# A state-space branch moved behind each step's evacuation, with a staging tile for its cosine product, two recurrence buffers and a setup in smaller portions

## The chip, the cores and the metric

The kernel runs on one core of a Trainium2 chip. The metric is the time of one execution on the device in microseconds (us). Five engines work side by side, each through a queue of its own, in order: PE (TensorE: matmuls into PSUM), DVE (VectorE), ACT (ScalarE), POOL (GpSimd), and SP (SyncE), which here issues every DMA.

## What is computed

One layer of a streaming encoder: 1024 positions of 1024 channels in float32. An input projection feeds two mixers, a diagonal state-space model (S5) and a gated short convolution. Cut to what matters:

```python
proj = jnp.einsum('bsd,dn->bsn', x, w_in) + b_in
u, h, c_gate, b_gate, gate_a, gate_b = jnp.split(proj, [o1, o2, o3, o4, o5], axis=-1)
y_a = s5_ssm(u, ...)                      # 32 groups of 16 channels, 64 complex states each
g = jax.nn.gelu(y_a)
y_a = g * jax.nn.sigmoid(jnp.einsum('bsc,ce->bse', g, glu_w) + glu_b)
y_a = jnp.einsum('bsc,cd->bsd', y_a, w_ssm_out)
z = causal_depthwise_conv(c_gate * h, conv_w)
y_b = jnp.einsum('bsc,cd->bsd', b_gate * z, w_conv_out)
merged = jax.nn.sigmoid(gate_a) * y_a + jax.nn.sigmoid(gate_b) * y_b
x = layer_norm(ALPHA * x + jnp.einsum('bsd,de->bse', merged, w_o), ln1_g, ln1_b)
hid = jax.nn.silu(jnp.einsum('bsd,df->bsf', x, w_gate)) * jnp.einsum('bsd,df->bsf', x, w_up)
x = layer_norm(ALPHA * x + jnp.einsum('bsf,fd->bsd', hid, w_down), ln2_g, ln2_b)
```

The state of the S5 branch follows `x[t] = a * x[t-1] + B u[t]` with complex `a`, and `y = Re(C x) + D u`.

## The kernel before

**Matmuls.** Every operand is split into a rounded part and a remainder (`hi`, `lo`), and three products of them stand for one (L180 to L182). The large products use a seven-product scheme (Strassen's) on 2 x 2 blocks: a `Pair` of weight blocks gives seven *steps*, each of 12 matmuls of 128 x 512, into four PSUM banks. `Step` holds what belongs to a step: `add` (the sum of two weight blocks, on POOL unless told otherwise), `split` (two copies on ACT, the remainder on DVE), `mm` (the matmuls), and `after` (`Pair.ev`, the evacuation of what has become complete, on ACT, DVE and POOL).

**Order of the work.** All of it is written out by hand; nothing is reordered later. `run` (L310) walks over the steps. At step s it issues the add of step s+4, the split of step s+3, then a portion of each generator in the list `bg` that is due, then the matmuls of step s and its evacuation. A generator's `yield n` says that its next portion comes n steps later. Steps 0 to 111 are the input projection, 112 to 127 the convolution's output projection, 128 to 135 the gate of the S5 branch, 136 to 151 its output projection, and the feed-forward part follows.

**The branch.** The S5 branch lives in generators, beside steps 12 to 127:

- `setup` (L461) computes the tables of the transition `a` in many small DVE operations on 128 x 32 and 128 x 288 elements; `exp_to` is an exponential that is used twice. Its scratch `scr` lies in the tiles with the tags w, ws, z and zs.
- `mats(cc)`, `rot(cc)` and `flow(cc)` work on chunk cc, four groups of channels, cc = 0 to 7. `mats` builds matrices: B (`bst`), Cp, four transposes into the small PSUM tile `pst`, and the kernel product into the small PSUM tile `pk` (L648), copied into K, from which eight DMAs fill the matrix T. `rot` makes a table of cosines C and one of sines S.
- `flow(cc)` is the recurrence: a product into the small PSUM tile `psw` (L710); `w`, its copy by ACT; `ws`, w with its halves swapped by two DMAs; w becomes psw times C on DVE and ws becomes ws times S on POOL; their sum goes through a scan into z (L729); z is rotated back in the same way with `zs` (L733 to L736); the output product `psy` (L739 to L742) uses T and z, and its copy `yn` is stored. Then `s["y"]` is set, on which later chunks wait.
- `gelu(tl)` follows two chunks each.

There are two small PSUM buffers (tag sm, L604), used in turn by pst, pk, psw and psy. The staging ring `stage` (tag st, L338) has four places and is used by evacuations too.

**The end of the branch.** The last flow calls `load_v` (L747), which loads the convolution's result into the tiles z, zs, ws and bp. At the end of step 111, `begin_b` (L913) runs all generators on (`spin`, L1349) until these loads have been issued, and then splits the eight parts of v, which step 112 multiplies. `begin_glu` does the same ahead of step 128 until no generator is left.

Of the kernel before, what the change touches and what calls it, by code (L numbers as in the profile page):

```python
# [15 lines left out]
P = 128  # L16
# [31 lines left out]
def kernel(  # L48
# [256 lines left out]
    def flush():  # L305
        todo, later[:] = later[:], []
        for f in todo:
            f()

    def run(lo, hi):  # L310
        for s in range(lo, hi):
            for f in steps[s].pre:
                f()
            if s + 4 < len(steps) and steps[s + 4].add:
                steps[s + 4].add(eng=V if steps[s + 4].addv else G)
            if s + 3 < len(steps) and steps[s + 3].split:
                steps[s + 3].split()
            for it in list(bg):
                if it[1] <= s:
                    try:  # L320
                        it[1] = s + max(1, next(it[0]) or 1)
                    except StopIteration:
                        bg.remove(it)
            steps[s].mm()
            flush()
            for f in steps[s].mid + steps[s].after:
                f()

    def start(gen, s=0):
        bg.append([gen, s])  # L330
# [121 lines left out]
    def stile(shape, tag, nm, bufs=1, dt=F32):  # L452
        return nonlocal_state["p"].tile(shape, dt, tag=tag, name=nm, bufs=bufs)
# [7 lines left out]
    def setup():  # L461
# [10 lines left out]
        sMim = tb["sMim"] = stile([P, NG, 8], "sMim", "sMim")  # L472
        E8 = tb["E8"] = stile([P, NG], "E8", "E8")
        ph8 = tb["ph8"] = stile([P, 2, NG], "ph8", "ph8")
        scr = [stile([P, 4 * P], t, f"scr_{t}") for t in ("w", "ws", "z", "zs")]
        used = [0] * 4

        def carve(*shape):
            n = int(np.prod(shape))
            i = min(i for i in range(4) if used[i] + n <= 4 * P)  # L480
            t = scr[i][:, used[i] : used[i] + n]
            used[i] += n
            return t.rearrange("p (a b) -> p a b", a=shape[0]) if len(shape) == 2 else t
# [9 lines left out]
        def exp_to(o, y):  # L493
            m, r, q = carve(NG), carve(NG), carve(NG)
            ts(r, y, -100.0, 90.0, ALU.max, ALU.min)
            ts(m, r, LOG2E, MAGIC, ALU.mult, ALU.add)
            ts(m, m, MAGIC, -127.0, ALU.subtract, ALU.max)
            V.tensor_scalar_min(m, m, 128.0)
            V.scalar_tensor_tensor(r, m, -LN2_1, r, ALU.mult, ALU.add)
            V.scalar_tensor_tensor(r, m, -LN2_2, r, ALU.mult, ALU.add)  # L500
            V.tensor_scalar_mul(q, r, 1.0 / 5040.0)
            for c in (1.0 / 720.0, 1.0 / 120.0, 1.0 / 24.0, 1.0 / 6.0, 0.5, 1.0):
                V.scalar_tensor_tensor(q, q, c, r, ALU.add, ALU.mult)
            ts(it, m, 127.0, 8388608.0, ALU.add, ALU.mult)
            V.scalar_tensor_tensor(o, q, 1.0, it.bitcast(F32), ALU.add, ALU.mult)
            yield 1
# [10 lines left out]
        mul(E[:, :, 3:5], E[:, :, 1:3], E[:, :, 2:3].to_broadcast([P, NG, 2]))  # L517
        mul(E[:, :, 5:9], E[:, :, 1:5], E[:, :, 4:5].to_broadcast([P, NG, 4]))
        V.tensor_copy(E8, E[:, :, 8])
        th, hh, hl = carve(NG), carve(NG), carve(NG)  # L520
        mul(th, li, dt)
        V.tensor_scalar_mul(hl, th, 4097.0)
# [14 lines left out]
        add(phh, phh, tm[:, 2])  # L537
        add(phh, phh, tm[:, 3])
        wrap(phh, th)
        add(phl, pr[:, 3], pr[:, 2])  # L540
        add(phl, phl, pr[:, 1])
        add(phl, phl, pr[:, 0])
# [14 lines left out]
        yield 1  # L557
        mul(nLre, nLre, E)
        mul(Lim, Lim, E)
        den, fr, fi, nr, tp = carve(NG), carve(NG), carve(NG), carve(NG), carve(NG)  # L560
        mul(den, lr, lr)
        mul(tp, li, li)
# [49 lines left out]
    def mats(cc):  # L612
# [34 lines left out]
        for g in range(4):  # L647
            PE.matmul(pk[0:16, g, :], B[:, g, 7, :], Cp[:, g, 0:8, :].rearrange("p n c -> p (n c)"),  # L648
                      start=True, stop=True)
        K = stile([16, 4, P], "yn", f"K{cc}")  # L650
        S.activation(K, pk[0:16], AF.Copy)
        for g in range(4):
            V.scalar_tensor_tensor(K[:, g, 0:16], ident[0:16, 0:16], tb["dss"][:, g0 + g : g0 + g + 1],
# [49 lines left out]
    def flow(cc):  # L703
# [8 lines left out]
        S.activation(w, ps, AF.Copy)  # L712
        ws = stile([P, 4, P], "ws", f"ws{cc}")
        swap(ws, w)
        s["sin"] = True
        yield 2
        c = slice(0, 127)
        mul(ws[:, :, c], ws[:, :, c], s["S"], G)
        mul(w[:, :, c], ps[:, :, c], s["C"])
        yield 1  # L720
        add(w[:, :, c], w[:, :, c], ws[:, :, c])
        while cc and "y" not in st[cc - 1]:
            yield 1
        z = stile([P, 4, P], "z", f"z{cc}")
        zs = stile([P, 4, P], "zs", f"zs{cc}")
        V.memset(zs[:, :, 0:1], 0.0)
        S.activation(zs[:, :, 1:P], tb["E8"][:, 4 * cc : 4 * cc + 4, None].to_broadcast([P, 4, 127]), AF.Copy)
# [6 lines left out]
        mul(z[:, :, c], z[:, :, c], s["C"])  # L734
        yield 1
        sub(z[:, :, c], z[:, :, c], zs[:, :, c])  # L736
        yield 3
        ps = small(f"psy{cc}")
        for g in range(4):  # L739
            PE.matmul(ps[:, g, :], s["T"][:, g], s["UT"][:, g], start=True, stop=False)  # L740
# [157 lines left out]
    def load_v(k):  # L898
        if k not in vrs:
            if k == 2:  # L900
                vrs[k] = epi.tile([P, 10, P], F32, tag="zE", name=f"vr{k}")[:, 0:8].rearrange("p a b -> p (a b)")
            elif k == 3:
                vrs[k] = wring.tile([P, KT, P], F32, tag="raw", name=f"vr{k}", bufs=4).rearrange("p a b -> p (a b)")
            else:
                vrs[k] = [stile([P, 4, P], t, f"vr_{t}").rearrange("p a b -> p (a b)")
                          for t in (("z", "zs"), ("ws", "bp"))[k]]
                for h in range(2):
                    nc.sync.dma_start(vrs[k][h], v_d[k, :, half(h)])
                return
            nc.sync.dma_start(vrs[k], v_d[k])  # L910
            vrs[k] = [vrs[k][:, half(h)] for h in range(2)]
# [736 lines left out]
```

## Time and profile before

| | |
|---|---|
| median of 3 runs | 1306.01 us (1303.51 to 1306.93) |
| the profiled execution's own time | 1304.74 us |
| its span, first to last instruction | 1302.9 us |
| mean granted clock of PE | 0.981 |
| moved by DMA | 148.75 MB, mean 114 GB/s |

The profile is of one execution. It gives busy times by engine, the waits (engine and line that waited, engine and line that ended the wait, then the sum in us, how often, and the longest), a timeline (start and duration in us, engine, line, operation, output <- inputs, and in brackets the idle time ahead and what ended it), and windows (start and end, their length, then the busy time and count of PE, of PE's weight loads, of DVE, ACT and POOL, then PE's granted clock, the share of the DMA engines and GB/s). Queue rows name the queue, the size of a transfer and the median time from issue to landing. A PE that stands still between two stretches of dense matmuls shows as idle time ahead of a matmul.

### The profile page before, as it was taken

How to read it: one execution, taken by the hardware profiler on the slowest of the kernel's cores; microseconds unless marked ns; L12 is line 12 of the kernel's file. 1: busy time of each engine (PE TensorE's matmuls, PEld its weight loads, DVE VectorE, ACT ScalarE, POOL GpSimd, SP SyncE). 2: the span in 40 equal slices, each digit the busy share in tenths (PEclk: the TensorE clock that was granted, in tenths of full speed). 3: DMA queues.
4: the chain of work that ended last, by engine and by line, in shares of the span. 5: the costliest groups of instructions: out<-in, count | busy, mean ns of one | idle time of the engine just before them, and what ended most of it. 6: DMA issues, size and time to landing. Idle time of an engine off the chain costs nothing. (4 is left out here: it accounts for less than half of the span.)

```text
span 1302.9 us, 16504 instructions
## 1 busy us (share of the span) xinstructions
PE 1210.6 (93%) x5365; PEld 979.4 (75%) x5365; DVE 860.4 (66%) x1321; ACT 765.4 (59%) x1320; POOL 777.8 (60%) x577
## 2 busy tenths in 40 slices
PE   6788899899899999999879999999999997999984
PEld 4566687777687888888658888888888875877764
DVE  6988688786676675689984444444444445566888
ACT  5645767788786252243435555555555567777871
POOL 5826878696861135123876565566556547585856
PEclk9899999999999999999989999999999998999998
DMA  5221342444456536124214323222215349420012
GB/s 196 78 88 45 110 122 82 128 157 142 131 151 230 195 116 237 38 97 162 81 49 153 104 92 98 73 73 97 95 52 162 97 137 360 143 64 1 1 49 81
DMA packets 95414, 148.75 MB, mean 114 GB/s; under 512 B 16736, under 2 KB 48480, under 8 KB 95072
## 3 DMA queue, kind: packets, MB, share of 16 engines
q1 hardware_dynamic: 95328, 147.70, 35.2%
q8 instruction: 43, 0.70, 0.2%
q14 instruction: 43, 0.35, 0.1%
HBM read 106.11 MB, written 36.18 MB: 109 GB/s over the span
## 5 line engine op out<-in xcount | busy, mean ns | idle before, releaser
L180 PE MATMUL ps_f<-x1h,wl_f 128*128 128x512 f32 x616 | 241.5, 392 | 12.1 <-DVE wl_f L115 7.7
L181 PE MATMUL ps_f<-x1l,wh_f 128*128 128x512 f32 x616 | 240.6, 391 | 2.1 <-DVE x1l L115 2.1
L182 PE MATMUL ps_f<-x1h,wh_f 128*128 128x512 f32 x616 | 240.5, 390 | 0.0
L180 PEld LDWEIGHTS ps_f<-x1h,wl_f 128*128 128x128 f32 x616 | 116.1, 189 | 39.0 <-issue 8.5
L181 PEld LDWEIGHTS ps_f<-x1l,wh_f 128*128 128x128 f32 x616 | 116.1, 188 | 26.7 <-DVE x1l L115 2.7
L182 PEld LDWEIGHTS ps_f<-x1h,wh_f 128*128 128x128 f32 x616 | 116.0, 188 | 24.3
L1478 PE MATMUL pe<-rBh,rAl 128*128 128x512 f32 x297 | 119.0, 401 | 15.4 <-ACT rBh L138 6.4
L115 DVE TENSOR_TENSOR wl_f<-t_f,hp 128x512 fp32r<-128x512 f32 x92 | 62.9, 684 | 88.8 <-ACT hp L137 88.8
L1479 PE MATMUL pe<-rBl,rAh 128*128 128x512 f32 x297 | 116.8, 393 | 0.6 <-DVE rBl L115 0.6
L1480 PE MATMUL pe<-rBh,rAh 128*128 128x512 f32 x297 | 116.5, 392 | 0.0
L180 PE MATMUL ps_gt<-xh,wl_gt 128*128 128x512 f32 x224 | 90.5, 404 | 3.9 <-DVE ec_hc L112 1.4
L182 PE MATMUL ps_gt<-xh,wh_gt 128*128 128x512 f32 x224 | 88.8, 396 | 0.0
L181 PE MATMUL ps_gt<-xl,wh_gt 128*128 128x512 f32 x224 | 88.5, 395 | 0.0
L106 POOL TENSOR_TENSOR tB<-B,B 128x512 f32<-128x512 f32 x55 | 71.8, 1307 | 27.9 <-DVE rBl L115 16.3
L106 POOL TENSOR_TENSOR tA<-A,A 128x512 f32<-128x512 f32 x54 | 69.8, 1297 | 29.9 <-DVE rAl L115 7.4
L106 POOL TENSOR_TENSOR t_f<-raw_f,raw_f 128x512 f32<-128x512 f32 x62 | 83.5, 1347 | 6.6 <-DVE wl_f L115 6.6
L1478 PEld LDWEIGHTS pe<-rBh,rAl 128*128 128x128 f32 x297 | 56.2, 189 | 35.4 <-ACT rBh L138 11.4
L138 ACT ACTIVATE wh_f<-t_f 128x512 fp32r<-128x512 f32 x92 | 57.4, 624 | 32.0 <-PE ps_f L182 31.9
L137 ACT ACTIVATE hp<-t_f 128x512 fp32r<-128x512 f32 x92 | 55.3, 601 | 31.9 <-POOL t_f L106 30.1
L109 POOL TENSOR_TENSOR sgf<-sgf,eb_f 128x512 f32<-128x512 f32 x21 | 27.6, 1313 | 70.7 <-ACT sgf L1183 70.7
L1479 PEld LDWEIGHTS pe<-rBl,rAh 128*128 128x128 f32 x297 | 56.3, 190 | 12.3 <-DVE rBl L115 1.3
L1480 PEld LDWEIGHTS pe<-rBh,rAh 128*128 128x128 f32 x297 | 56.3, 190 | 11.3
(414 smaller groups left out, 3270.1 us busy)
## 6 DMA issues: line engine op xcount, KB each, us to landing
raw_f<-in_wgu SPq DMA_DIRECT2D x45, 512.0 KB, 3.9
h_d<-hid SPq DMA_DIRECT2D x44, 256.0 KB, 2.4
B<-in_wd SPq DMA_DIRECT2D x44, 256.0 KB, 6.1
A<-h_d SPq DMA_DIRECT2D x44, 256.0 KB, 5.8
raw_gt<-in_w SPq DMA_DIRECT2D x16, 512.0 KB, 4.1
s_d<-sg SPq DMA_DIRECT2D x32, 256.0 KB, 2.5
sgd<-s_d SPq DMA_DIRECT2D x16, 512.0 KB, 3.6
raw_hc<-in_w SPq DMA_DIRECT2D x8, 512.0 KB, 4.5
```

What stands on the lines that cost most here:

```text
L106: eng.tensor_tensor(o, a, b, op)
L109: eng.tensor_tensor(o, a, b, ALU.mult)
L115: eng.tensor_tensor(o, a, b, ALU.subtract)
L137: S.activation(hp, raw, AF.Copy)
L138: S.activation(hi, raw, AF.Copy)
L180: PE.matmul(ps, self.lo[:, k, :], xh[:, k, :], start=first and k == 0, stop=False, skip_group_check=True)
L181: PE.matmul(ps, self.hi[:, k, :], xl[:, k, :], start=False, stop=False, skip_group_check=True)
L182: PE.matmul(ps, self.hi[:, k, :], xh[:, k, :], start=False, stop=last and k == 3, skip_group_check=True)
L1478: PE.matmul(ps, al[:, c], bh, start=kp == 0, stop=False)
L1479: PE.matmul(ps, ah[:, c], bl, start=False, stop=False)
L1480: PE.matmul(ps, ah[:, c], bh, start=False, stop=kp == NK - 1)
```

## The change

Five edits, all in the S5 branch and in the loop that issues it:

1. In `run`, the portions of `bg` are issued behind the matmuls and the evacuation of step s, no longer ahead of them.
2. In `flow`, the cosine product follows psw at once, in the same portion, and goes into a tile `wc` of the staging ring; before, it overwrote w two steps later. The sum reads wc and ws and writes w.
3. z gets two buffers, and the scan of a chunk waits for `rotated` (the last chunk's rotation back has been issued) in place of `y`. The pause ahead of psy is four steps, before three.
4. Five pauses more in `setup`, counting the one in `exp_to` twice.
5. K lies in the staging ring, no longer in a tile of its own.

```diff
--- before.py
+++ after.py
@@ -315,16 +315,16 @@
                 steps[s + 4].add(eng=V if steps[s + 4].addv else G)
             if s + 3 < len(steps) and steps[s + 3].split:
                 steps[s + 3].split()
+            steps[s].mm()
+            flush()
+            for f in steps[s].mid + steps[s].after:
+                f()
             for it in list(bg):
                 if it[1] <= s:
                     try:
                         it[1] = s + max(1, next(it[0]) or 1)
                     except StopIteration:
                         bg.remove(it)
-            steps[s].mm()
-            flush()
-            for f in steps[s].mid + steps[s].after:
-                f()
 
     def start(gen, s=0):
         bg.append([gen, s])
@@ -472,7 +472,7 @@
         sMim = tb["sMim"] = stile([P, NG, 8], "sMim", "sMim")
         E8 = tb["E8"] = stile([P, NG], "E8", "E8")
         ph8 = tb["ph8"] = stile([P, 2, NG], "ph8", "ph8")
-        scr = [stile([P, 4 * P], t, f"scr_{t}") for t in ("w", "ws", "z", "zs")]
+        scr = [stile([P, 4 * P], t, f"scr_{t}", 2 if t == "z" else 1) for t in ("w", "ws", "z", "zs")]
         used = [0] * 4
 
         def carve(*shape):
@@ -498,6 +498,7 @@
             V.tensor_scalar_min(m, m, 128.0)
             V.scalar_tensor_tensor(r, m, -LN2_1, r, ALU.mult, ALU.add)
             V.scalar_tensor_tensor(r, m, -LN2_2, r, ALU.mult, ALU.add)
+            yield 1
             V.tensor_scalar_mul(q, r, 1.0 / 5040.0)
             for c in (1.0 / 720.0, 1.0 / 120.0, 1.0 / 24.0, 1.0 / 6.0, 0.5, 1.0):
                 V.scalar_tensor_tensor(q, q, c, r, ALU.add, ALU.mult)
@@ -517,6 +518,7 @@
         mul(E[:, :, 3:5], E[:, :, 1:3], E[:, :, 2:3].to_broadcast([P, NG, 2]))
         mul(E[:, :, 5:9], E[:, :, 1:5], E[:, :, 4:5].to_broadcast([P, NG, 4]))
         V.tensor_copy(E8, E[:, :, 8])
+        yield 1
         th, hh, hl = carve(NG), carve(NG), carve(NG)
         mul(th, li, dt)
         V.tensor_scalar_mul(hl, th, 4097.0)
@@ -537,6 +539,7 @@
         add(phh, phh, tm[:, 2])
         add(phh, phh, tm[:, 3])
         wrap(phh, th)
+        yield 1
         add(phl, pr[:, 3], pr[:, 2])
         add(phl, phl, pr[:, 1])
         add(phl, phl, pr[:, 0])
@@ -557,6 +560,7 @@
         yield 1
         mul(nLre, nLre, E)
         mul(Lim, Lim, E)
+        yield 1
         den, fr, fi, nr, tp = carve(NG), carve(NG), carve(NG), carve(NG), carve(NG)
         mul(den, lr, lr)
         mul(tp, li, li)
@@ -647,7 +651,7 @@
         for g in range(4):
             PE.matmul(pk[0:16, g, :], B[:, g, 7, :], Cp[:, g, 0:8, :].rearrange("p n c -> p (n c)"),
                       start=True, stop=True)
-        K = stile([16, 4, P], "yn", f"K{cc}")
+        K = stage(f"K{cc}").rearrange("p (g k) -> p g k", g=4)[0:16]
         S.activation(K, pk[0:16], AF.Copy)
         for g in range(4):
             V.scalar_tensor_tensor(K[:, g, 0:16], ident[0:16, 0:16], tb["dss"][:, g0 + g : g0 + g + 1],
@@ -712,16 +716,16 @@
         S.activation(w, ps, AF.Copy)
         ws = stile([P, 4, P], "ws", f"ws{cc}")
         swap(ws, w)
-        s["sin"] = True
+        c = slice(0, 127)
+        wc = stage(f"wc{cc}").rearrange("p (g k) -> p g k", g=4)
+        mul(wc[:, :, c], ps[:, :, c], s["C"])
         yield 2
-        c = slice(0, 127)
         mul(ws[:, :, c], ws[:, :, c], s["S"], G)
-        mul(w[:, :, c], ps[:, :, c], s["C"])
-        yield 1
-        add(w[:, :, c], w[:, :, c], ws[:, :, c])
-        while cc and "y" not in st[cc - 1]:
+        yield 1
+        add(w[:, :, c], wc[:, :, c], ws[:, :, c])
+        while cc and "rotated" not in st[cc - 1]:
             yield 1
-        z = stile([P, 4, P], "z", f"z{cc}")
+        z = stile([P, 4, P], "z", f"z{cc}", 2)
         zs = stile([P, 4, P], "zs", f"zs{cc}")
         V.memset(zs[:, :, 0:1], 0.0)
         S.activation(zs[:, :, 1:P], tb["E8"][:, 4 * cc : 4 * cc + 4, None].to_broadcast([P, 4, 127]), AF.Copy)
@@ -734,7 +738,8 @@
         mul(z[:, :, c], z[:, :, c], s["C"])
         yield 1
         sub(z[:, :, c], z[:, :, c], zs[:, :, c])
-        yield 3
+        s["rotated"] = True
+        yield 4
         ps = small(f"psy{cc}")
         for g in range(4):
             PE.matmul(ps[:, g, :], s["T"][:, g], s["UT"][:, g], start=True, stop=False)
@@ -902,7 +907,7 @@
             elif k == 3:
                 vrs[k] = wring.tile([P, KT, P], F32, tag="raw", name=f"vr{k}", bufs=4).rearrange("p a b -> p (a b)")
             else:
-                vrs[k] = [stile([P, 4, P], t, f"vr_{t}").rearrange("p a b -> p (a b)")
+                vrs[k] = [stile([P, 4, P], t, f"vr_{t}", 2 if t == "z" else 1).rearrange("p a b -> p (a b)")
                           for t in (("z", "zs"), ("ws", "bp"))[k]]
                 for h in range(2):
                     nc.sync.dma_start(vrs[k][h], v_d[k, :, half(h)])
```

Three places in the order of instructions show what moves. First DVE, around the cosine product of the first chunk (cc = 0; cp is already the second chunk's, for its pk; wl_hc are splits; vs, ec and eb are evacuations of the projection; the scan is listed as a SCALAR_TENSOR_TENSOR at L729, L733 with the change). Before:

```order
L115 TENSOR_TENSOR wl_hc_2_1378<-t_hc_2_1331,hp_1379 128x512
L115 TENSOR_TENSOR cp_1342<-cp_1342,ct_1343 128x576
L385 SCALAR_TENSOR_TENSOR vs_1_1399<-ps_b_1_1283,b1s,hs_710 128x512
L112 TENSOR_TENSOR ec_b_1328<-ps_b_1_1283,ec_b_1328 128x512
L115 TENSOR_TENSOR wl_hc_5_1406<-t_hc_5_1375,hp_1407 128x512
L109 TENSOR_TENSOR w_1351<-psw_1346,ctab_1087 128x4x127
L112 TENSOR_TENSOR eb_b_1296<-ps_b_2_1315,eb_b_1296 128x512
L115 TENSOR_TENSOR wl_hc_1_1427<-t_hc_1_1403,hp_1428 128x512
L112 TENSOR_TENSOR w_1351<-w_1351,ws_1353 128x4x127
L726 MEMSET zs_1441 128x4
L729 SCALAR_TENSOR_TENSOR z_1440<-zs_1441,w_1351 128x512
```

With the change:

```order
L109 TENSOR_TENSOR cp_1478<-nLre,bc_1286 128x576
L109 TENSOR_TENSOR wc_1492<-psw_1482,ctab_1221 128x4x127
L115 TENSOR_TENSOR wl_hc_7_1500<-t_hc_7_1451,hp_1501 128x512
L115 TENSOR_TENSOR cp_1478<-cp_1478,ct_1479 128x576
L115 TENSOR_TENSOR wl_hc_6_1528<-t_hc_6_1497,hp_1529 128x512
L106 TENSOR_TENSOR eb_hc_1472<-ps_hc_0_1423,ea_hc_1439 128x512
L115 TENSOR_TENSOR wl_hc_2_1551<-t_hc_2_1525,hp_1552 128x512
L112 TENSOR_TENSOR ec_hc_1518<-ps_hc_1_1459,ec_hc_1518 128x512
L112 TENSOR_TENSOR w_1487<-wc_1492,ws_1489 128x4x127
L730 MEMSET zs_1579 128x4
L733 SCALAR_TENSOR_TENSOR z_1578<-zs_1579,w_1487 128x512
```

Before, the product into w stands behind the subtraction of cp, two splits and two evacuations; now the product into wc stands ahead of that subtraction and of the splits, and the sum and the scan follow directly behind an evacuation of their step (ec_hc).

Second DVE at the end of the projection, from the last chunk's rotation (before) or from its sum (after) to the first split of v (vl). The names gl and gy are of the GELU, wl_so the weights of step 112 and later, eb_gt and ec_gt evacuations of the last pair:

```order
L109 TENSOR_TENSOR z_3573<-z_3573,ctab_3193 128x4x127
L115 TENSOR_TENSOR wl_gt_3_3680<-raw_gt_0_3457,hp_3681 128x512
L775 SCALAR_TENSOR_TENSOR gy_1_3504<-gl_1_3570,gy_1_3504 128x512
L115 TENSOR_TENSOR z_3573<-z_3573,zs_3574 128x4x127
L115 TENSOR_TENSOR wl_gt_7_3707<-t_gt_7_3677,hp_3708 128x512
L115 TENSOR_TENSOR wl_gt_6_3733<-t_gt_6_3704,hp_3734 128x512
L106 TENSOR_TENSOR eb_gt_3701<-ps_gt_0_3655,ea_gt_3671 128x512
L115 TENSOR_TENSOR wl_so_1_0_3755<-raw_so_1_3621,wh_so_1_0_3754 128x512
L112 TENSOR_TENSOR ec_gt_3725<-ps_gt_1_3688,ec_gt_3725 128x512
L115 TENSOR_TENSOR wl_so_1_0_3797<-raw_so_1_3673,wh_so_1_0_3796 128x512
L112 TENSOR_TENSOR eb_gt_3701<-ps_gt_2_3712,eb_gt_3701 128x512
L115 TENSOR_TENSOR vl<-vr_z,vh 128x512
```

With the change:

```order
L112 TENSOR_TENSOR eb_gt_3658<-ps_gt_2_3672,eb_gt_3658 128x512
L112 TENSOR_TENSOR w_3696<-wc_3701,ws_3698 128x4x127
L730 MEMSET zs_3775 128x4
L733 SCALAR_TENSOR_TENSOR z_3774<-zs_3775,w_3696 128x512
L772 SCALAR_TENSOR_TENSOR gl_1_3771<-gl_1_3771,gy_1_3729 128x512
L109 TENSOR_TENSOR z_3774<-z_3774,ctab_3411 128x4x127
L115 TENSOR_TENSOR z_3774<-z_3774,zs_3775 128x4x127
L780 SCALAR_TENSOR_TENSOR gy_1_3729<-gl_1_3771,gy_1_3729 128x512
L115 TENSOR_TENSOR vl<-vr_z,vh 128x512
```

Before, four splits of weights and three evacuations lie between the rotation's subtraction and vl; now the sum, the scan, the rotation and vl follow each other with only the GELU between.

Third SP, the DMA queue, at the same place (yn is stored to y_d, sg are gates, raw_so weights). Before:

```order
L392 DMA s_d<-sg_1_0_3750 128x512
L745 DMA y_d<-yn_3767 128x512
L908 DMA vr_z<-v_d 128x512
L908 DMA vr_zs<-v_d 128x512
L908 DMA vr_ws<-v_d 128x512
L908 DMA vr_bp<-v_d 128x512
L392 DMA s_d<-sg_0_1_3790 128x512
```

With the change:

```order
L705 DMA zs_3775<-z_3774 64x512
L392 DMA s_d<-sg_0_0_3794 128x512
L750 DMA y_d<-yn_3806 128x512
L782 DMA g_d<-gy_1_3729 128x512
L750 DMA y_d<-yn_3826 128x512
L913 DMA vr_z<-v_d 128x512
L913 DMA vr_zs<-v_d 128x512
L913 DMA vr_ws<-v_d 128x512
L913 DMA vr_bp<-v_d 128x512
```

The swap of z for the last chunk (zs) now stands four rows ahead of the first load of v, with the stores of the last two chunks' yn between; before, it stood twelve rows ahead of it, above this piece.

## The prediction

> **What bounds the kernel now.** I read the page's totals first, then the windows, then the waits of PE (TensorE) for the stretch that the change touches, then the timeline at the longest of these waits.
>
> ```profile
> PE 1210.6 (93%) x5365; PEld 979.4 (75%) x5365; DVE 860.4 (66%) x1321; ACT 765.4 (59%) x1320; POOL 777.8 (60%) x577
> ```
>
> PE is the bound: it is busy for 93% of the span, and no other engine is above 66%. A saved microsecond therefore counts only where PE stands still or is clocked down. The branch work runs from the start of step 14 (67 us) to the start of step 112 (408 us). There the windows say:
>
> ```profile
> 67.00:408.00 341.00, 312.63 (x1465) 252.40 (x1464) 257.28 (x416) 240.36 (x406) 233.80 (x184) 0.98 0.40 121
> ```
>
> PE is busy for 312.6 of 341 us, so 28.4 us of standing still is all that reordering can win there, apart from the clock. PE's waits in the same stretch account for nearly all of it:
>
> ```profile
> PE pk L648 <- DVE w L109: 11.8, 4, 5.6
> PE psy L741 <- DVE z L115: 3.9, 3, 1.5
> PE ps_hc L180 <- DVE ec_hc L112: 3.3, 1, 3.3
> PE pst L642 <- ACT gy L768: 2.1, 1, 2.1
> PE ps_hc L180 <- ACT ec_hc L233: 1.9, 1, 1.9
> PE ps_gt L180 <- DVE ec_hc L112: 1.4, 1, 1.4
> PE ps_gt L180 <- ACT eb_gt L230: 1.0, 1, 1.0
> PE pk L648 <- DVE cp L115: 1.0, 1, 1.0
> PE ps_gt L180 <- ACT ea_gt L227: 0.8, 1, 0.8
> ```
>
> They fall into three groups. The kernel product pk waits 11.8 us for the cosine product w on DVE. Main matmuls (ps_hc, ps_gt) wait 3.3 + 1.9 + 1.4 + 1.0 + 0.8 = 8.4 us for a late evacuation, which holds their PSUM bank. The rest, psy, pst and pk for cp, is 3.9 + 2.1 + 1.0 = 7.0 us. The longest wait in full:
>
> ```profile
> 157.40 0.39 PE L181 MATMUL ps_b<-xl,wh_b 128*128 128x512 f32 x1
> 157.63 0.39 PE L182 MATMUL ps_b<-xh,wh_b 128*128 128x512 f32 x1
> 158.69 1.68 DVE L115 TENSOR_TENSOR cp<-cp,ct 128x576 f32<-128x576 f32 x1
> 162.76 0.68 DVE L109 TENSOR_TENSOR w<-psw,ctab 128x508 f32<-128x508 f32 x1
> 163.59 0.80 PE L648 MATMUL pk<-cp,bst 128*16 128x128 f32 x3 [5.57 <-DVE w L109]
> ```
>
> Two things are to be seen. Main matmuls start 0.23 us apart, so a step of twelve is 2.76 us. And pk waited for the small PSUM buffer that psw had filled and that only the cosine product frees. DVE comes to that product late, since it stands two steps behind psw in its queue, after splits and evacuations.
>
> **What goes.** *Cosine product.* It now stands directly behind psw and writes a staging tile, so that it need not wait until the swap has read w. Its 0.68 us is the same work as before, and the buffer is free some three steps before its next user, the pk that follows four steps behind psw. The next late thing at 157.63 is cp, ready at 158.69 + 1.68 = 160.4, some 2.3 us after PE was free. I let those 2.3 us stand: 11.8 - 2.3 = **9.5 us** go (bounds 6, if DVE is late with cp elsewhere too, and 11.8).
>
> *The clock behind it.* The granted clock fell after the two longest of these waits:
>
> ```profile
> 163.50:167.30 3.80, 3.71 (x13) 2.57 (x14) 3.70 (x5) 3.64 (x7) 2.95 (x3) 0.50 0.00 0
> 356.20:361.70 5.50, 5.41 (x17) 3.85 (x18) 4.82 (x6) 4.75 (x9) 5.42 (x5) 0.50 0.13 48
> 86.80:90.20 3.40, 0.15 (x1) 0.00 (x0) 3.19 (x13) 1.15 (x2) 1.31 (x1) 1.00 0.00 0
> ```
>
> It was 0.50 for 3.8 and for 5.5 us. Work at half clock takes twice its time, so half of each is lost: 1.9 and 2.8 us, **4.7 us** together; both go with the waits (bound below: 2.8). The third row is a standstill of 3.3 us that kept a clock of 1.00. The Trainium skill, TensorE: Matmul & The Clock Gate, section on the HAM clock gate, has a rule here: an idle window of about 3.4 us halves the clock, and a busy one of about 3.4 us restores it. By its figure each dip would be estimated at 1.7 us, 3.4 for both, and the sum of what goes at 1.3 us less; the rows agree on the border (3.3 us kept the clock, longer waits lost it) and give more, so the sum goes by the rows. The rule speaks against this change in one place, the drain below.
>
> *Late evacuations.* They are late because a portion of branch work stands ahead of them. The setup is the worst:
>
> ```profile
> 86.81 1.58 DVE L112 TENSOR_TENSOR scr_ws<-scr_ws 128x32 f32<-128x32 f32 x3
> 89.52 0.68 DVE L112 TENSOR_TENSOR ec_hc<-ps_hc,ec_hc 128x512 f32<-128x512 f32 x1
> 90.26 0.50 PE L180 MATMUL ps_hc<-xh,wl_hc 128*128 128x512 f32 x1 [3.31 <-DVE ec_hc L112]
> ```
>
> DVE works through small setup operations without a gap while the evacuation of a full bank stands behind them. With the evacuation ahead of the portion and the portion cut, it can be late only by what the previous portion overran. I take three quarters of 8.4, **6.3 us** (bounds 3 and 8.4). The 7.0 us of psy, pst and cp I count as unchanged: the output product is one portion later, but all portions come one place later, so again three steps of matmuls lie between the last subtraction on z and psy (bounds: -3, one more microsecond at each of the three psy waits; +4, those 3.9 us gone). The second z buffer and the earlier release of the scan save latency in the chain of chunks, not PE time. Setup portions add no instruction.
>
> Sum of what goes: 9.5 + 4.7 + 6.3 = **20.5 us** (bounds 6 + 2.8 + 3 - 3 = 9 and 11.8 + 4.7 + 8.4 + 4 = 29).
>
> **What comes: the drain ahead of step 112.** The five new pauses in the setup put the first chunk's transposes six steps later (behind step 39, before step 34), and the fourth pause ahead of psy adds one step to every two chunks. psw of the last chunk moves from before step 99 to behind step 107. The scan of the last chunk is issued behind step 110, and begin_b, at the end of step 111, cannot wait: it runs the branch on until the two loads of v are issued. Everything from the scan to those loads then stands with one step of matmuls beside it. Before, the same chain was spread over steps 105 to 111:
>
> ```profile
> 384.00 2.09 DVE L729 TENSOR_TENSOR_SCAN z<-zs,w 128x512 f32<-128x512 f32 x1
> 389.27 1.20 POOL L109 TENSOR_TENSOR zs<-zs,stab 128x508 f32<-128x508 f32 x1 [4.26 <-DMA zs<-z]
> 374.73 0.68 DVE L115 TENSOR_TENSOR z<-z,zs 128x508 f32<-128x508 f32 x1
> 398.38 0.38 PE L740 MATMUL psy<-ut,T 128*128 128x128 f32 x2
> 400.08 0.48 PE L180 MATMUL ps_gt<-xh,wl_gt 128*128 128x512 f32 x1
> 400.36 0.60 ACT L744 ACTIVATE yn<-psy 128x512 f32<-128x512 f32 x1 [0.53 <-PE psy L741]
> 401.41 0.43 SPq L908 DMA_DIRECT2D vr_z<-v_d  x1
> 407.79 0.63 ACT L121 ACTIVATE vh<-vr_z 128x512 fp32r<-128x512 f32 x1 [0.46 <-DMA vr_z<-v_d]
> 408.47 0.50 PE L180 MATMUL pso<-vh,wl_so 128*128 128x512 f32 x1
> ```
>
> From the end of step 110, called E: DVE evacuates a bank and adds w (twice 0.68), clears a column and starts the scan, about E + 1.7. From scan to sine product took 384.00 to 389.27, 5.3 us, swap included; the product is 1.2, the subtraction 0.7: psy at E + 9.0. From psy over its copy, the store, the load of v and its split to the first pso took 398.38 to 408.47, 10.1 us: pso at E + 19.1. Without a standstill it would start at E + 2.76 + twice 1.7 for two psy (398.38 to 400.08), E + 6.2. PE stands still for 12.9 us, and a dip of the clock behind so long a wait costs 1.9. I take 1.0 off because the queue is emptier:
>
> ```profile
> gr<-g_d SPq DMA_DIRECT2D x6, 256.0 KB, 4.4
> vr_z<-v_d SPq DMA_DIRECT2D x1, 256.0 KB, 6.4
> 255.66 1.23 DVE L729 TENSOR_TENSOR_SCAN z<-zs,w 128x512 f32<-128x512 f32 x1 [0.80 <-ACT zs L727]
> ```
>
> That is 12.9 + 1.9 - 1.0 = 13.8, **14 us**. Its bounds: 11 with a load of 4.4 us and no dip; 19 where the scan also waits for ACT's copy into zs, as in the third row but behind the square of a GELU whose own load is late (0.8 there, 1.8 allowed), and the clock falls twice (1.9 + 2.8). The page of the skill named above would estimate 1.7 for each dip; none of the ends is taken from it. What is queued behind: on DVE the eight splits of v and the last evacuation of step 111, on SP the store of y and then the loads of v, on PE step 112 itself.
>
> K and wc take two more places in the staging ring of four. K is held until its eight DMAs have landed, so a sigmoid may wait for it on ACT for a microsecond or two; the bank it evacuates is needed four steps (11 us) later, and I count nothing.
>
> **Sum.** The profiled execution took 1304.74 us, 1.8 more than its span. 1304.7 - 20.5 + 14 = **1298.2 us**. The median shown is 1306.01, 1.3 above that execution; I leave the forecast at the profiled one's level. Two kernels of this length can be told apart from about 0.3%, 3.9 us: 1302.1 to 1309.9 is "same".
>
> **The rivals.** *The drain is mostly covered* and more of the waits go: 26 us gained, 11 lost, 1290 us. For it: in a quiet queue the loads land in 4.4 us. Against it: each link of the drain waits for the one before it.
>
> *The waits only move.* If half of the 20.5 comes back as waits for cp, bst or z, since DVE, ACT and POOL are as loaded as before, it is 1304.7 - 10.3 + 14 = 1308 us. So the change would do its work on w, and the rest would be given back at step 112. For it: cp was ready at 160.4 only, 2.3 us late. Against it, the second of the two longest waits:
>
> ```profile
> 350.94 0.88 DVE L115 TENSOR_TENSOR cp<-cp,ct 128x576 f32<-128x576 f32 x1
> 356.30 1.86 PE L648 MATMUL pk<-cp,bst 128*16 128x128 f32 x8 [3.40 <-DVE w L109]
> ```
>
> There cp was ready at 351.8, before PE began to wait at 352.9.
>
> *Slower: the adds on POOL.* Branch work now stands behind the evacuation and ahead of the next add, which feeds ACT's copies:
>
> ```profile
> ACT hp L137 <- POOL t_gt L106: 23.3, 15, 3.3
> 354.16 1.27 POOL L115 TENSOR_TENSOR ec_gt<-ec_gt,ea_gt 128x512 f32<-128x512 f32 x1
> 355.38 1.28 POOL L106 TENSOR_TENSOR t_gt<-raw_gt 128x512 f32<-128x512 f32 x1
> 360.54 2.08 POOL L112 TENSOR_TENSOR ctab<-ctab,ang 128x508 f32<-128x508 f32 x1
> ```
>
> ACT already waits 23.3 us for such adds. From the end of a step: ACT's copy 0.6, POOL's evacuation add 1.3, two branch operations of 1.2 to 2.1, the add 1.3, ACT's two copies 1.2, DVE's split 0.7: 7.5 to 9.3 us against four steps, 11 us. It decides once POOL falls more than 2 to 3 us behind; then PE waits for weights once or twice per chunk, 8 chunks times 2 us, and the time is 1298.2 + 16 = 1314 us. Against it: POOL was busy for 233.8 of 341 us here.
>
> **How the numbers follow.** Forecast 0.46 (1290 to 1303 by itself), drain covered 0.13, waits only move 0.25, slower 0.16. Nearly all of the first two lies below 1302.1: faster 0.57. The third gives same 0.27 with the edge of the first, and the last 0.16. The range leaves out the bounds' far ends on both sides: 1286 to 1312.
>
> **What would show it.** Right: no wait of pk for w or wc, no half clock near chunks 1 and 7, waits of ps_hc and ps_gt below 3 us together, and one standstill of 12 to 15 us ahead of the first pso, in which scan, swap, sine product, psy, store and load of v follow each other. Wrong: a first pso within 6 us of the last ps_gt; pk waiting for cp or bst in several chunks; ps_gt waiting for wl_gt.

## The result, and the profile after

| | before | after |
|---|---|---|
| median of four runs each | 1305.37 us (1303.51 to 1306.93) | 1322.44 us (1318.70 to 1323.67) |
| the profiled execution | 1304.74 us | 1323.61 us |
| its span | 1302.9 us | 1321.8 us |
| mean granted clock of PE | 0.981 | 0.977 |

After divided by before is 1.0132, with an interval of 1.0119 to 1.0146: the changed kernel is slower by 17 us, above the upper end of the forecast's range. The totals on the page of the changed kernel:

```profile
PE 1215.7 (92%) x5365; PEld 980.8 (74%) x5365; DVE 863.8 (65%) x1321; ACT 768.0 (58%) x1322; POOL 776.5 (59%) x577
```

The number of matmuls is the same, and PE is busy for 5.1 us longer in a span 18.9 us longer, so most of the loss is standing still. To find where, I cut the trace at three marks: the first ps_hc (start of step 14), the last ps_gt (end of step 111) and the first pso (start of step 112). Windows of the changed kernel (start and end, length, busy time and count of PE, its weight loads, DVE, ACT, POOL, then clock, DMA share and GB/s):

```profile
66.11:400.41 334.30, 308.75 (x1432) 245.07 (x1431) 257.47 (x409) 238.63 (x401) 229.97 (x182) 1.00 0.37 115
400.41:423.80 23.39, 5.76 (x34) 5.22 (x32) 4.83 (x9) 4.61 (x8) 2.85 (x2) 0.72 0.55 176
...
408.00:414.00 6.00, 0.00 (x0) 0.00 (x0) 2.36 (x5) 1.44 (x3) 1.68 (x1) 0.50 0.43 131
```

Before, the first stretch (67.19 to 408.19) took 341.0 us and the second 0.3 us. So the middle became 6.7 us shorter and the drain 23.1 us longer. But 32 matmuls fewer stand in the middle: the output products psy of the last two chunks, twice 1.7 = 3.4 us of PE's work, went behind it. The middle gained 6.7 - 3.4 = 3.3 us, where the forecast had 20.5; the drain cost 23.1 - 3.4 = 19.7 us, where it had 14. What remains of the 18.9 us lies outside the two stretches.

**The middle.** PE's waits from the first ps_hc to the last ps_gt, changed kernel (waiting line, what ended the wait, sum, times, longest; rows under 0.7 us are left out):

```profile
PE ps_gt L180 <- DVE wl_gt L115: 10.6, 13, 1.9
PE ps_b L180 <- DVE wl_b L115: 3.0, 2, 1.6
PE ps_hc L180 <- DVE eb_hc L112: 2.1, 1, 2.1
PE ps_gt L180 <- ACT eb_gt L230: 1.3, 1, 1.3
PE ps_gt L180 <- DVE ec_hc L112: 1.2, 1, 1.2
PE ps_hc L180 <- ACT ea_hc L227: 1.2, 1, 1.2
PE ps_gt L180 <- ACT wh_gt L138: 1.1, 1, 1.1
PE ps_b L180 <- ACT ec_b L233: 1.0, 1, 1.0
PE ps_gt L180 <- ACT hp L376: 0.9, 1, 0.9
PE ps_gt L180 <- DVE eb_hc L112: 0.8, 1, 0.8
PE ps_gt L180 <- ACT ea_gt L227: 0.7, 1, 0.7
```

All waits of pk, psy and pst are gone, 18.8 us by the rows of before. The late evacuations are still there: 2.1 + 1.3 + 1.2 + 1.2 + 1.0 + 0.8 + 0.7 = 8.3 us in other places, against 8.4. And a kind is here that the list of before did not have at all: main matmuls that wait for their own weights, 10.6 + 3.0 + 1.1 = 14.7 us. PE idles for 334.30 - 308.75 = 25.6 us, before for 28.4. The longest of the new waits in the timeline of the changed kernel:

```profile
250.93 1.31 POOL L106 TENSOR_TENSOR t_gt<-raw_gt,raw_gt 128x512 f32<-128x512 f32 x1
251.05 1.74 DVE L694 SCALAR_TENSOR_TENSOR ang<-ctab 128x508 f32<-128x508 f32 x1
...
252.88 0.72 ACT L696 ACTIVATE ctab<-ang,sgn 128x508 f32<-128x508 f32 x1 [1.15 <-DVE ang L694]
253.51 0.58 ACT L137 ACTIVATE hp<-t_gt 128x512 fp32r<-128x512 f32 x1
...
254.12 0.69 DVE L115 TENSOR_TENSOR wl_gt<-t_gt,hp 128x512 fp32r<-128x512 f32 x1 [1.33 <-ACT hp L137]
...
254.87 0.50 PE L180 MATMUL ps_gt<-xh,wl_gt 128*128 128x512 f32 x1 [1.90 <-DVE wl_gt L115]
```

POOL's sum t_gt was ready at 250.93 + 1.31 = 252.24. ACT's copy hp of it starts at 253.51, since a branch instruction (the cosine of the table, L696) stands ahead of it in ACT's queue and itself waits 1.15 us for DVE. That holds the weights back for 1.3 of the 1.9 us of standstill; the other 0.6 us would be left, by the same rows, with the copy at once, because POOL's sum was late as well. A late evacuation before had the same form: a branch portion stood ahead of the projection's work on an in-order queue. Only the work that it delays has changed.

The longest wait is not typical. Of the 13 waits for weights of 0.6 us or more (14.1 us together), 7 (6.3 us) have a split that starts straight behind a branch operation on DVE, three times the new product into wc. In 4 (4.7 us) the copy hp waited for POOL's sum, and in 2 (3.1 us) it stood behind a branch instruction on ACT, as above. One of the seven:

```profile
350.03 0.60 ACT L137 ACTIVATE hp<-t_gt 128x512 fp32r<-128x512 f32 x1 [1.11 <-POOL t_gt L106]
...
350.48 1.78 DVE L115 TENSOR_TENSOR z<-z,zs 128x508 f32<-128x508 f32 x1
...
352.18 0.67 DVE L115 TENSOR_TENSOR wl_gt<-t_gt,hp 128x512 fp32r<-128x512 f32 x1
```

ACT's copy is done at 350.63, but DVE works on the branch's z until 352.26. The split follows, and PE starts at 352.91 behind a wait of 1.3 us.

**The drain.** The timeline of the changed kernel from the start of step 111:

```profile
397.78 0.50 PE L180 MATMUL ps_gt<-xh,wl_gt 128*128 128x512 f32 x1 [0.76 <-DVE wl_gt L115]
...
401.85 0.37 SPq L764 DMA_DIRECT2D gy<-y_d  x1
...
402.73 1.17 POOL L109 TENSOR_TENSOR ws<-ws,stab 128x508 f32<-128x508 f32 x1 [6.73 <-DMA ws<-w]
403.93 0.69 DVE L112 TENSOR_TENSOR w<-wc,ws 128x508 f32<-128x508 f32 x1 [3.20 <-POOL ws L109]
...
406.06 0.63 ACT L769 ACTIVATE gl<-gy 128x512 f32<-128x512 f32 x1 [6.97 <-DMA s_d<-sg]
406.59 0.61 ACT L731 ACTIVATE zs<-E 128x508 f32<-128x508 f32 x1
...
407.23 1.23 DVE L733 TENSOR_TENSOR_SCAN z<-zs,w 128x512 f32<-128x512 f32 x1 [2.60 <-ACT zs L731]
...
411.65 1.68 POOL L109 TENSOR_TENSOR zs<-zs,stab 128x508 f32<-128x508 f32 x1 [7.76 <-DMA zs<-z]
413.37 0.69 DVE L115 TENSOR_TENSOR z<-z,zs 128x508 f32<-128x508 f32 x1 [1.06 <-POOL zs L109]
...
414.11 0.80 PE L746 MATMUL psy<-z,cp 128*128 128x127 f32 x2 [11.30 <-DVE z L115]
...
417.50 0.60 ACT L749 ACTIVATE yn<-psy 128x512 f32<-128x512 f32 x1 [7.23 <-PE psy L746]
...
418.54 0.38 SPq L913 DMA_DIRECT2D vr_z<-v_d  x1
...
423.12 0.63 ACT L121 ACTIVATE vh<-vr_z 128x512 fp32r<-128x512 f32 x1 [5.02 <-DMA vr_z<-v_d]
423.80 0.80 PE L180 MATMUL pso<-vh,wl_so 128*128 128x512 f32 x1 [6.34 <-ACT vh L121]
```

The chain is the one that the forecast named, link by link. From scan to first pso it took 423.80 - 407.23 = 16.6 us, forecast 17.4. What was wrong is its start. Step 110 ended at 397.02, and step 111 began at 397.78 behind a wait for its weights; the scan was forecast 1.7 us behind the end of step 110 and came 10.2 us behind it. The swap of w had only just been issued and its product on POOL could not start before 402.73. Its matmuls psw had ended long before, at 385.49:

```profile
384.44 1.05 PE L714 MATMUL psw<-ut,bp 128*128 128x128 f32 x8
...
393.83 0.59 ACT L716 ACTIVATE w<-psw 128x512 f32<-128x512 f32 x1
...
396.57 0.32 SPq L782 DMA_DIRECT2D g_d<-gy  x1
396.98 0.52 SPq L704 DMA_DIRECT2D ws<-w  x1
```

ACT's copy into w came 8.3 us behind psw (5.3 us before the change), with ACT at work all that time on branch instructions, splits and evacuations, two table loads of 1.28 us among them. On SP the swap then stood behind the store of a GELU's result, which DVE had ready at 396.53. So w was late in the same way as the weights in the middle, behind other work on in-order queues. Then the scan waited 2.6 us more for ACT's copy into zs, which stood behind the square of a GELU (L769) that sat until 406.06. It reads gy, whose load was issued at 401.85; the label names another DMA. PE stood still for 11.3 and 6.3 us, and the windows row above shows the clock at 0.50 from 408.

### The profile page after: what moved, and what is told of

Its sections match the earlier page's. It is cut to its first block, busy times and chain, and to the rows that moved or that the text cites. A ratio compares the mean times of both kernels' runs of the same rounds, so it can differ in the third digit from the quotient of the medians.

```text
span 1321.8 us, 16531 instructions
## 1 busy us (share of the span) xinstructions
PE 1215.7 (92%) x5365; PEld 980.8 (74%) x5365; DVE 863.8 (65%) x1321; ACT 768.0 (58%) x1322; POOL 776.5 (59%) x577
## 5 line engine op out<-in xcount | busy, mean ns | idle before, releaser
L180 PE MATMUL ps_gt<-xh,wl_gt 128*128 128x512 f32 x224 | 91.0, 406 | 17.2 <-DVE wl_gt L115 10.6
L1483 PEld LDWEIGHTS pe<-rBh,rAl 128*128 128x128 f32 x297 | 56.5, 190 | 34.5 <-ACT rBh L138 11.1
L180 PEld LDWEIGHTS ps_gt<-xh,wl_gt 128*128 128x128 f32 x224 | 42.1, 188 | 33.7 <-DVE wl_gt L115 15.3
```

What stands on the lines that cost most here:

```text
L180: PE.matmul(ps, self.lo[:, k, :], xh[:, k, :], start=first and k == 0, stop=False, skip_group_check=True)
L1483: PE.matmul(ps, al[:, c], bh, start=kp == 0, stop=False)
```

## The experiments

Each ratio is to the kernel before, measured beside it on the same chip (its medians: 1304.95 us for the first four, 1304.59 for the next, 1304.13 for the last). "The middle" and "the drain" are the two stretches cut as above; before they took 341.0 and 0.3 us.

### First four: which part costs, which gains

**e1_no_pauses**: the changed kernel without the five pauses.

```diff
             V.scalar_tensor_tensor(r, m, -LN2_2, r, ALU.mult, ALU.add)
-            yield 1
...
         V.tensor_copy(E8, E[:, :, 8])
-        yield 1
...
         wrap(phh, th)
-        yield 1
...
         mul(Lim, Lim, E)
-        yield 1
```

> The changed kernel with the five pauses in the setup taken out again: the branch runs five steps earlier, so its end has five steps (13.8 us) more cover ahead of step 112. If the drain ahead of step 112 is what made the change slower (19.6 us of PE standing still there), about 8 us of it remain (store, load and split of v) and the time falls by 10 to 13 us, to 1309 to 1312. If the time was lost elsewhere, by the new order of the portions, it stays above 1317.

**e2_ahead**: the changed kernel with the portions of `bg` ahead of the matmuls again (edit 1 undone).

> The changed kernel with the portions issued ahead of the step's matmuls again; all other edits stay. The drain stays, one step shorter. If the order is what took the expected gain in the middle (PE's waits for wl_gt and wl_b, 13.6 us, are new with the change), these waits go and the time falls by 10 to 15 us, to 1307 to 1312. If the order costs nothing in the middle, only the step of the drain shows: 1318 to 1322, or more where evacuations come late again.

**e3_product_only**: the kernel before, with the cosine product at once and in a staging tile (edit 2 alone).

```diff
-        s["sin"] = True
-        yield 2
         c = slice(0, 127)
+        wc = stage(f"wc{cc}").rearrange("p (g k) -> p g k", g=4)
+        mul(wc[:, :, c], ps[:, :, c], s["C"])
+        yield 2
         mul(ws[:, :, c], ws[:, :, c], s["S"], G)
-        mul(w[:, :, c], ps[:, :, c], s["C"])
         yield 1
-        add(w[:, :, c], w[:, :, c], ws[:, :, c])
+        add(w[:, :, c], wc[:, :, c], ws[:, :, c])
```

> The kernel before with one edit alone: the cosine product directly behind psw, into a staging tile. If its waits were worth what the prediction counted, 9.5 us and 4.7 us of clock go and no drain comes: about 1291. If the waits only move to cp, bst and z, 1299 to 1304.

**e4_behind_only**: the kernel before, with the portions behind matmuls and evacuation (edit 1 alone).

> The kernel before with one edit alone: portions behind the evacuation. The branch ends one step later than before, psy of the last chunk ahead of step 110. If the order helps, late evacuations (8.4 us) go and the time falls to 1298 to 1301. If it delays the splits of the weights by as much as it wins or more, PE waits for wl_gt and wl_b appear and the time is 1305 to 1315.

| | median us | ratio [interval] | middle, drain us |
|---|---|---|---|
| e1_no_pauses | 1306.92 | 1.0015 [1.0005, 1.0026] | 334.3, 9.0 |
| e2_ahead | 1323.49 | 1.0139 [1.0115, 1.0163] | 342.3, 18.1 |
| e3_product_only | 1303.14 | 0.9991 [0.9981, 1.0001] | 341.5, 0.2 |
| e4_behind_only | 1306.80 | 1.0017 [1.0005, 1.0029] | 342.0, 1.7 |

The pauses cost 1322.44 - 1306.92 = 15.5 us, more than the 10 to 13 us expected and nearly all of the loss, and the drain falls without them from 23.4 to 9.0 us.

The order within a step is worth nothing in time: undone (e2), the time is that of the changed kernel within about 1 us; alone (e4), it costs 1.8 us. But it decides what PE waits for. In e2's middle the waits for weights are 3.1 us, not 14.7, and the late evacuations 19.1 us, not 8.3. One row of each kind:

```profile
PE ps_gt L180 <- ACT ea_gt L227: 8.1, 3, 5.1
...
PE ps_gt L180 <- DVE wl_gt L115: 1.3, 2, 0.8
```

e2's middle is 8.0 us longer than the changed kernel's, 1.7 of it one psy more, and its drain, with the branch one step earlier, 5.3 us shorter.

And e3 shows what became of the largest gain of the forecast. PE's waits in its middle:

```profile
PE psy L741 <- DVE z L115: 5.5, 4, 2.4
PE ps_gt L180 <- ACT ea_gt L227: 4.3, 1, 4.3
PE pk L648 <- DVE cp L115: 3.6, 3, 2.5
```

The 11.8 us of pk for w are gone, as the edit says. In their place pk waits 3.6 us for cp (before 1.0), psy 5.5 for z (3.9), and an evacuation 4.3 (0.8): 7.7 of the 11.8 us came back under these three names. The clock also still falls, behind other waits: its mean in the middle is 0.98, as before. Of 9.5 + 4.7 us counted for this edit, 1.8 us came, with an interval that includes none.

### Next four: what paces the middle, and the late scan

Three kernels without pauses and with three steps ahead of psy, so that no drain disturbs: **e5_no_pauses_y3** itself; **e6_heavier**, which wraps the angles of `rot` a second time with the same result (two more ACT instructions and one more on POOL per chunk); **e7_lighter**, which leaves the second wrap out.

```diff
 e5_no_pauses_y3, against e1_no_pauses
-        yield 4
+        yield 3
         ps = small(f"psy{cc}")
 e6_heavier, against e5_no_pauses_y3
         awrap()
+        awrap()
         yield 1
 e7_lighter, against e5_no_pauses_y3
         yield 1
-        awrap()
         yield 1
```

> The changed kernel without the five pauses in the setup and with three steps, not four, ahead of psy: psy of the last chunk then stands ahead of step 110, two steps before the convolution's output projection. If the drain is a matter of steps, its remaining 9 us (last ps_gt to first pso in the run without pauses) shrink to 1 or 2 and the time falls by 6 to 8 us against that run, to 1299 to 1301. If the fourth step was needed, psy waits for z and the time stays at 1305 or more.

> The kernel e5_no_pauses_y3 with the second wrap of the angles done twice in each chunk (the result is the same): 2 more activations on ACT (1.4 us) and one more subtraction on POOL (1.3 us) per chunk, 11 and 10 us in all. If PE's waits in the middle come from the other engines being late in their queues, whatever PE waits for by name, the time rises by 3 to 10 us. If the waits belong to single chains (w, cp, z) that this work isn't part of, within 2 us.

> The kernel e5_no_pauses_y3 without the second wrap of the angles (left out, so the rotations are less exact or wrong): 11 us less on ACT and 10 us less on POOL over the eight chunks. If PE's waits in the middle come from the other engines being late in their queues, the time falls by 3 to 10 us. If the waits belong to single chains, within 2 us.

**e8_zs_pool**: the changed kernel, with the copy into zs on POOL.

```diff
-        S.activation(zs[:, :, 1:P], tb["E8"][:, 4 * cc : 4 * cc + 4, None].to_broadcast([P, 4, 127]), AF.Copy)
+        G.tensor_copy(zs[:, :, 1:P], tb["E8"][:, 4 * cc : 4 * cc + 4, None].to_broadcast([P, 4, 127]))
```

> The changed kernel with the copy of E8 into zs on POOL, no longer on ACT. If the scan of the last chunk is late because that copy stands on ACT behind the GELU's square, which waits for a load, the scan starts about 2.6 us earlier and the time falls by 2 to 4 us, to 1318 to 1320. If the drain hangs on the swap of w alone, within 1.5 us of 1322.

| | median us | ratio [interval] | middle, drain us |
|---|---|---|---|
| e5_no_pauses_y3 | 1307.01 | 1.0016 [1.0005, 1.0028] | 341.4, 1.4 |
| e6_heavier | 1324.00 | 1.0149 [1.0134, 1.0164] | 358.0, 2.1 |
| e7_lighter | 1302.81 | 0.9989 [0.9979, 1.0000] | 336.7, 2.8 |
| e8_zs_pool | 1317.58 | 1.0101 [1.0086, 1.0116] | 333.3, 20.8 |

The windows of the middle, of e5, then e6, then e7:

```profile
65.86:407.27 341.41, 316.44 (x1465) 253.46 (x1463) 253.47 (x416) 237.19 (x404) 231.97 (x184) 0.98 0.40 122
```

```profile
66.18:424.20 358.02, 319.08 (x1465) 253.46 (x1463) 256.02 (x416) 248.24 (x420) 240.93 (x192) 0.98 0.38 115
```

```profile
67.00:403.69 336.69, 313.44 (x1464) 251.57 (x1463) 250.82 (x416) 226.06 (x387) 221.27 (x176) 0.99 0.41 122
```

PE has the same matmuls to do in all three. The time rises by 17.0 us in e6, more than the 3 to 10 expected, and falls by 4.2 in e7. In e6 ACT is busy 11.1 us and POOL 9.0 us more, and the middle grows by 16.6 us; in e7 they are busy 11.1 and 10.7 us less, and it shrinks by 4.7. So PE, busy for 93%, is paced in this stretch by queues of which ACT's is busy for 69% and POOL's for 68% (of e5's 341.4 us). What the runs don't separate is ACT from POOL, nor the amount of work from the length of the portion; DVE, busy for 74%, was not varied.

e5 against e1 shows a second thing. With psy one step earlier the drain falls from 9.0 to 1.4 us, the middle grows from 334.3 to 341.4 us, and the time is the same, where 6 to 8 us less were expected. The psy that now stands in the middle is 1.7 of these 7.1 us. For the rest, PE stands still for 25.0 us, not 21.8, and its other matmuls are drawn busy for 2.2 us longer; why is not shown. A short middle is no gain by itself: middle and drain have to be taken together.

e8 takes 4.9 us off the changed kernel by the medians, and about 4 by the ratios (1.0101 against 1.0132). Two rows of its timeline, step 111 having begun at 395.59:

```profile
402.53 1.23 DVE L733 TENSOR_TENSOR_SCAN z<-zs,w 128x512 f32<-128x512 f32 x1
...
409.29 0.80 PE L746 MATMUL psy<-z,cp 128*128 128x127 f32 x2 [8.66 <-DVE z L115]
```

The scan starts 6.9 us behind the start of step 111, not 9.4, without a wait for zs. So ACT's copy into zs holds 2.5 us of the delay, and the late swap the rest.

### Last four: the drain without its chain

**e9_loads**: the changed kernel, with both loads of v issued ahead of the last scan, behind the sum into w, into tiles free by then.

```diff
         add(w[:, :, c], wc[:, :, c], ws[:, :, c])
+        if cc == 7:
+            load_v(0)
+            load_v(1)
...
         s["y"] = True
-        if cc == 7:
-            load_v(0)
-            load_v(1)
...
-                vrs[k] = [stile([P, 4, P], t, f"vr_{t}", 2 if t == "z" else 1).rearrange("p a b -> p (a b)")
-                          for t in (("z", "zs"), ("ws", "bp"))[k]]
+                if k == 0:
+                    vrs[k] = [stile([P, 4, n, 16], t, f"vr_{t}").rearrange("p a b c -> p (a b c)")[:, 0:512]
+                              for t, n in (("bst", 8), ("gt", 9))]
+                else:
+                    vrs[k] = [stile([P, 4, P], t, f"vr_{t}").rearrange("p a b -> p (a b)") for t in ("bp", "ws")]
```

> The changed kernel with the loads of v moved up: issued behind the last chunk's sum, into tiles that are free by then (bst, gt, bp, ws), no longer behind the last psy. If the standstill ahead of step 112 comes from begin_b waiting for those loads, the first pso starts within 6 us of the last ps_gt (23.4 us in the changed kernel). The last psy then comes seven steps later, and the GELU behind it no longer fits ahead of step 128, so part of the drain shows again there: 1308 to 1316. If the standstill has another cause, the time stays above 1319.

**e10_loads_np**: e9 without the five pauses. **e11_loads_np_zs**: e10 with the copy into zs on POOL. **e12_pauses_only**: the kernel before with the five pauses (edit 4 alone).

> The same, without the five pauses in the setup: the GELU fits ahead of step 128. Against the run without pauses (1306.9, 9.0 us from last ps_gt to first pso) the 7 us of drain go and nothing takes their place: 1298 to 1302, faster than before. If the middle gives it back, 1304 to 1308.

> The same, with the copy of E8 into zs on POOL, no longer on ACT. If what is left of PE's waits in the middle is ACT and DVE being late in their queues, the time falls by 2 to 4 us against the run without this edit. If POOL is the late one, it rises.

> The kernel before with one edit alone: the five pauses in the setup. The last psw moves from step 99 to 104, so the last psy cannot come before step 112 and a drain appears. If the drain is the change's cost, 1311 to 1317; if it takes the other edits too, 1302 to 1306.

| | median us | ratio [interval] | middle, drain us |
|---|---|---|---|
| e9_loads | 1317.65 | 1.0103 [1.0084, 1.0123] | 333.4, 8.6 |
| e10_loads_np | 1301.05 | 0.9975 [0.9965, 0.9984] | 333.4, 2.5 |
| e11_loads_np_zs | 1301.72 | 0.9982 [0.9972, 0.9991] | 336.3, 1.2 |
| e12_pauses_only | 1305.69 | 1.0016 [1.0007, 1.0026] | 331.0, 11.8 |

In e9 the drain falls by 14.8 us, to 8.6 where less than 6 was expected, but the time by 4.8 only. The rest comes back at step 128, where `begin_glu` runs the generators to their end in the same way. Its windows and its waits of PE there:

```profile
440.00:470.00 30.00, 25.43 (x92) 18.82 (x91) 17.65 (x24) 10.65 (x19) 6.15 (x4) 0.83 0.43 146
```

```profile
PE psg L180 <- ACT gh L121: 2.4, 2, 1.4
PE psg L181 <- DVE gl L115: 2.2, 3, 1.1
```

PE idles for 30.00 - 25.43 = 4.6 us there, and the clock is 17% short of 30 us, up to 5.1 us more: about the 10.0 us that are missing. The starts of PE's work agree: the first pso comes 15.6 us earlier than in the changed kernel (408.18 against 423.80), the first psg 12.4 us (457.61 against 469.99), the last psg only 4.1 us (487.51 against 491.57). The changed kernel has nothing of the kind around its step 128, which begins at 470:

```profile
470.00:500.00 30.00, 30.00 (x134) 24.81 (x133) 22.15 (x31) 16.91 (x30) 7.85 (x6) 1.00 0.44 148
```

A branch that is late stays late: with the first drain shortened, the second takes most of the gain. In the changed kernel, the long first drain gave the branch the time that it needed.

Without pauses (e10) both are nearly gone, and this is the fastest of all, 3.1 us below the kernel before:

```profile
67.01:400.43 333.42, 312.74 (x1448) 250.32 (x1447) 256.38 (x415) 236.41 (x402) 232.82 (x184) 0.98 0.39 123
400.43:402.91 2.48, 0.40 (x3) 0.00 (x1) 1.12 (x3) 1.29 (x3) 0.00 (x0) 0.97 1.05 394
```

Middle and drain are 335.9 us together, 5.4 below before; one psy, 1.7 us, is done after them. Moving the zs copy to POOL as well (e11) gains nothing once no drain waits for it. ACT is busy there for 232.9 us of the middle, not 236.4, and POOL for 237.4, not 232.8, so a late ACT alone does not set the pace. The pauses alone (e12) cost 1.6 us, a tenth of the 15.5 that they cost beside the other edits: the middle is short, with a part of the branch behind it, and a drain of 11.8 us gives it back. The pauses alone put the last psw to step 104, the other edits alone (e1) to step 103; together they put it to step 108, with no more room to be late.

## Why the prediction was wrong

**The step that failed most: what goes, 20.5 us.** It added up waits as if each were a price of its own. The edits did what they say: no wait of pk for w or wc is left, no half clock near chunks 1 and 7, no wait of psy or pst in the middle. But the waits of ps_hc and ps_gt, forecast below 3 us together, are about 20 us. The idle time is set elsewhere, and the waits are where it shows. 18.8 us of small-PSUM waits went, and 14.7 us of waits for weights came. PE's idle time in the middle lies between 20 us (e12) and 28 us (before) in all of these kernels but e6 (39 us), whatever the names. e3 shows it for the largest term by itself, e6 and e7 show that work on ACT and POOL sets it, and in 7 of the 13 waits for weights the branch work ahead stands on DVE.

- *Cosine product, 9.5 us, and the clock behind it, 4.7 us*: the wait went, the time did not (e3: 1.8 us). The dips went too in the changed kernel; there PE's busy time fell by 3.9 us, of which the two moved psy are 3.4. So hardly anything of the 4.7 us is seen as won. In which small gaps it went is open: a matmul is drawn 0.39 us long and the next starts 0.23 us behind, so that a gap below 0.16 us doesn't show as idle.
- *Late evacuations, 6.3 us*: none of it came. 8.3 us of such waits are there, in other places. The new order did shorten them, 8.3 us against 19.1 with the order undone (e2), but the portions now stand ahead of the splits, and the waits for weights grew from 3.1 to 14.7 us.
- *psy, pst and cp, 7.0 us, counted as unchanged*: they went, all 7.0, more than the bound of 4 allowed. That was worth as little.

**The drain, 14 us: right in mechanism and order, too small.** It measured 19.7 us, just above the upper bound of 19. The term that was mis-sized is the start of the scan, forecast 1.7 us behind the end of step 110 and measured 10.2. The text had named the wait for zs behind a GELU's late load, and allowed 1.8 us for it; it was 2.6. The lateness of w it put at nothing. psw stood three steps ahead, but ACT's copy came 8.3 us behind it, so that the swap of w, issued at 396.98, was as exposed as the swap of z, which the forecast did count. The sign of one standstill of 12 to 15 us became two, of 11.3 and 6.3.

**The rivals.** *The waits only move* was true of the middle, and by more than the half that it allowed. *Slower: the adds on POOL* had the right sign, ps_gt waiting for wl_gt, but the wrong queue for most of it. In the changed kernel's waits of ACT the row for POOL's adds fell from 23.3 us to

```profile
ACT hp L137 <- POOL t_gt L106: 16.6, 9, 3.7
```

and POOL's adds came last in 4 of the 13 waits for weights only; in 7 it was branch work on DVE, in 2 on ACT. The outcome is the two together, with a larger drain: 3.3 us won and 19.7 lost give 1304.7 + 16.4 = 1321 us, against 1323.6 of the profiled execution.

**What stays open.** How the pace of the middle splits between ACT, DVE and POOL, and whether they slow each other: the subtraction on z takes 1.78 us at 350.48 and 0.69 us at 413.37, for the same shapes, and no run shows why. Also open is whether splits issued one more step ahead would take the waits for weights away, which was not tried.

## What to carry to other kernels

When the tightest engine waits for many different things by a microsecond or two each, do not add up the waits: look for the in-order queues behind them, and test by adding or removing work there, before counting any wait as a gain. Spreading side work over more steps delays its end; ask first what stands at its end, and whether the next phase must run it out with the main engine idle. If it must, take whatever the next phase needs (here the loads of v) out of that chain, and check the next such place, which inherits the delay.

## What the runs showed of the hardware beyond that

- Work added to engines that are busy for about 70% of a stretch can cost PE more than either engine got: 11.1 us on ACT and 9.0 us on POOL cost 16.6 us, while 11.1 and 10.7 us less gained 4.7. The price was not symmetric here.
- The clock fell to 0.50 within the 11.3 us standstill, and pairs of psy's matmuls behind it (from 414.70) are drawn 0.63 to 0.64 us long, where pairs at 400.64 to 402.43 took 0.38 to 0.39 us. The Trainium skill, TensorE: Matmul & The Clock Gate, section on the HAM clock gate, says that an idle window of about 3.4 us halves the clock; the row from 408 us agrees. Here the half clock fell on the drain that the change had made.
